# First and last groups of the prompt attention placed among the dense products beside them

## The chip, the cores and the metric

The kernel runs on one core of a Trainium2 chip. The metric is the device time of one execution in microseconds (us). The kernel before takes 2291.44 us, the median of 3 runs (2286.28 to 2295.47). One execution was also profiled; every instruction of that execution is in its trace.

## What is computed

The reference is one step of a decoder with two layers. It takes a prompt of 2048 tokens (width 1024) and a sample of 8 sequences of 4 new tokens each, whose past of 2048 tokens lies in a paged cache of keys and values (128 pages of 128 tokens, 4 heads of 128).

```
h   = rmsnorm(x)
a   = HGRN2(h)            # gated linear recurrence, 4 heads of 128
b   = forgetting attention(h)   # 4 heads of 128
x1  = x + concat(a * silu(ga), b * silu(gb)) @ w_out_even      # layer 0
x2  = x1 + GLA(rmsnorm(x1)) @ w_out_odd                        # layer 1
y   = rmsnorm(x2)
# forgetting attention of the prompt, per head, query t and key s <= t:
logits = q.k * scale + c[t] - c[s]        # c: running sum of log forget values
out    = softmax(logits) @ v
# of the sample: the same against the pages of its own past and its own new rows
```

The outputs are y for prompt and sample, the new keys, values and log forget values, and the final states of the two recurrences.

## The kernel before, in words

**Products.** A float32 product is made of three f16 products (`mm3`, L623 to L627): high by high, high by low, low by high. `act` is the large buffer with the left operand, split into a high and a low f16 part. A dense unit is one slice of a projection, 256 columns wide, for half of the prompt (1024 tokens, `hf` 0 or 1) and the sample's few rows. In the token-major form (`proj_tm`, L638) a unit has four steps of two token tiles each, called pairs: a pair is 2 tiles by 8 pieces of the contraction by 3, 48 products into a PSUM tile `pt_...`. A last small step treats the sample's few rows.

**Stages.** `phase_even` (L1118) makes the projections of layer 0. For each half it runs 16 units through `staged` (L1262); the last two are the keys Bk1 and the values Bv1 of the attention. Values leave PSUM by an eviction into `Bvs` (L1070), which the SP queue stores to DRAM as `vd` (L1084). At each step of the units `ahead` (L1551) does a step of the sample's work on cached keys: the list `KEYS` says at which steps 1 MB of key pages (`kp`, four loads at L1522, with their page numbers read into registers by `TENSOR_LOAD` at L1514) is loaded on SP; two and three steps later DVE transposes it (`kt`, L1526), then PE makes the scores, and SP stores them (`scd`). When the half changes, eight transposing loads on SP bring the second half's normalised rows into `act` (`act<-xhl`, L535).

`phase_fox` (L1347) is the attention. `fox_prompt` (L1365) goes through 16 groups (h, G): head h, 512 queries G, over the keys 0 to 512(G+1). SP loads what a group needs (L1379 on: `q`, `k`, the row `cb` of running sums from `cbd`, `v`, the gate `fsg`). Then, for each 128 queries: PE scores `s` (L625 to L627), DVE adds the bias and takes the maximum (`mx`, L1412), ACT takes the exponential into `L` (L1420), POOL scales it (L1428), PE transposes it (`pt<-ident,L`, L1448), ACT and DVE split it into the f16 parts `th` (L1455) and `tl` (L1456), and PE multiplies it with the values (`fo`). The finished output is stored to DRAM as `yT` (L1473), from POOL's queue. `fox_sample` (L1598) does the sample's attention over the cached values: 128 loads of 256 KB (`pgcache_fox_v`) and 34 products steps `pv` (L1750).

`phase_odd` (L2040) begins with layer 0's output projection. A unit of it needs a 256-column slice of the weight, loaded raw as `wr_o` and split into `w_o` (`half_unit`, L325: lines L356, L359, L362 and L363), and the left operand: `yT` read back from DRAM in pieces of 256 tokens (`y_pieces`, L1828; 1 MB each into the buffers `yr`, of which there are two), scaled and split into `act` by ACT, POOL and DVE (L1847 to L1854). The first half's pieces 0 to 3 come from the groups G = 0 and 1, so they do not wait for the last group (3,3).

**What sets the order.** The stages are generators that yield their cost. `until(a, ta, b, tb)` and `mux` alternate two of them so that each has done the same share of its total; `until` ends with the second, and `mux` with both. In `phase_fox` the prompt (total 270000) and the sample (500000) alternate so. What is left of the prompt alternates by `mux` with `prepare()` (L2119), which loads the first output unit's weights, splits them, and splits the pieces 0 and 1. Only then the attention's pools are closed and the output units run (`dense(0, 3)`). From this program order a scheduler lays out each engine's own instruction stream, within the dependencies; the streams then run in order on the chip.

## Time and profile before

| | us |
|---|---|
| median of 3 runs | 2291.44 |
| the profiled execution | 2291.65 |
| span of its trace, first to last instruction | 2289.9 |
| last even unit's products (Bv1) end, prompt's scores begin | about 911.4 |
| sample's transposed output `ys` (end of the sample) | about 1202.4 |
| end of the prompt's last group, first output unit begins | about 1229 |

The profile is of that one execution. PE is the matrix engine (PEld its weight loads, which run beside it), DVE the vector engine, ACT the scalar engine, POOL the general-purpose engine, SP the queue that issues most DMAs. A row of the timeline gives the start, the length, the engine, the line, the operation and its output and input; in square brackets stands how long the engine sat idle before it, and on whom it waited. A row of the waits gives the sum, the count and the longest. Successive matrix products overlap, so that a product shown as 0.27 us long can start 0.11 us after the one ahead of it. PEclk is the clock that was granted to PE, as a share of full speed.

### The profile page before, as it was taken

What the parts mean: (1) busy time and instruction counts of PE and PEld (TensorE: products, weight loads), DVE (VectorE), ACT (ScalarE), POOL (GpSimd) and SP (SyncE); (2) the same over time, 40 slices, a digit from 0 to 9 for tenths busy, and PEclk for the clock granted to TensorE, in tenths of its full rate; (3) what the DMA queues carried; (4) which work ended last, traced back from release to release, by engine and by line L of the source; (5) the groups of instructions that cost most, each with busy time, mean ns of one, the idle gap of its engine ahead of it and who ended that gap; (6) DMA issues with size and microseconds to landing.
All of it is one profiled execution on the core that took longest, in us unless ns stands there. A gap on an engine that the chain in (4) does not pass through costs nothing.

```text
span 2289.9 us, 58071 instructions
## 1 busy us (share of the span) xinstructions
PE 2195.9 (96%) x23316; PEld 1569.0 (69%) x23316; DVE 1400.7 (61%) x3154; ACT 994.3 (43%) x2216; POOL 724.9 (32%) x787
## 2 busy tenths in 40 slices
PE   7999999999999999899999999999999999999998
PEld 5667667774575588455457888677677667567887
DVE  7767677735564466877776454366665655557454
ACT  5434434321221221566667353554644644555243
POOL 2233234100110111544445354154442422232232
PEclk9999999999999999999999999999999999999999
DMA  7444545796575475977735779324325421115554
GB/s 235 144 124 150 160 150 185 233 238 151 159 184 138 118 204 149 280 223 246 223 111 170 260 219 253 101 71 144 92 97 101 120 79 59 54 52 179 171 179 152
DMA packets 361984, 364.02 MB, mean 159 GB/s; under 512 B 108161, under 2 KB 305090, under 8 KB 357490
## 3 DMA queue, kind: packets, MB, share of 16 engines
q1 hardware_dynamic: 359570, 353.69, 52.7%
q0 software_dynamic: 2144, 6.62, 0.8%
q8 instruction: 183, 3.00, 0.6%
q14 instruction: 87, 0.71, 0.1%
HBM read 245.85 MB, written 97.47 MB: 150 GB/s over the span
## 4 chain that ended last, share of the span: by engine, by line
PE 42%; DVE 3%; ACT 2%; DMA 2%; POOL 2%; issue 1%; SPq 0%; POOLq 0%; DVEq 0%; ACTq 0%
PE pt_o L625 4%; PE pt_o L626 4%; PE pt_o L627 4%; PE pt_Cv L625 2%; PE pt_Cv L627 2%; PE pt_Cv L626 2%; PE o_C L909 1%; PE gl_C L756 1%; PE pt L1448 1%; POOL s_C L842 1%; PE py_C L728 1%; ACT L L1420 1%; DMA wr_o<-in_w_out_odd 1%; PE fo L626 0%; PE fo L627 0%
## 5 line engine op out<-in xcount | busy, mean ns | idle before, releaser
L625 PE MATMUL pt_o<-w_o,act 128*128 128x256 f16 x1024 | 279.4, 273 | 1.4 <-ACT sg1C L682 1.4
L626 PE MATMUL pt_o<-w_o,act 128*128 128x256 f16 x1024 | 279.7, 273 | 0.0
L627 PE MATMUL pt_o<-w_o,act 128*128 128x256 f16 x1024 | 279.3, 273 | 0.0
L625 PEld LDWEIGHTS <-act 128*128 128x128 f16 x2304 | 226.1, 98 | 42.3 <-issue 5.3
L626 PEld LDWEIGHTS <-act 128*128 128x128 f16 x2304 | 226.3, 98 | 31.3 <-issue 2.2
L627 PEld LDWEIGHTS <-act 128*128 128x128 f16 x2304 | 226.1, 98 | 31.4 <-issue 2.6
L789 POOL TENSOR_TENSOR kA<-kA,fA 128x512 f32<-128x512 f32 (+1 forms) x56 | 74.2, 1325 | 367.9 <-PE gl_A L756 307.5
L625 PE MATMUL pt_Cv<-w_Cv,act 128*128 128x256 f16 (+1 forms) x512 | 141.5, 276 | 0.9 <-DVE rh L1959 0.8
L627 PE MATMUL pt_Cv<-w_Cv,act 128*128 128x256 f16 (+1 forms) x512 | 141.4, 276 | 0.0
L626 PE MATMUL pt_Cv<-w_Cv,act 128*128 128x256 f16 (+1 forms) x512 | 141.3, 276 | 0.0
L1420 ACT ACTIVATE L<-L,nm,kc 128x512 f32<-128x512 f32 (+3 forms) x160 | 118.2, 741 | 39.4 <-DVE nm L1418 36.1
L1428 POOL TENSOR_SCALAR L<-L,nm 128x512 f32<-128x512 f32 (+3 forms) x160 | 98.2, 629 | 87.4 <-DVE nm L1424 33.7
L789 POOL TENSOR_TENSOR kC<-kC,fC 128x512 f32<-128x512 f32 (+1 forms) x56 | 81.8, 1461 | 136.6 <-PE gl_C L756 93.1
L1455 ACT ACTIVATE th<-pt 128x512 f16<-128x512 f32 (+3 forms) x159 | 80.9, 526 | 74.1 <-PE pt L1448 73.4
L1526 DVE STREAM_TRANSPOSE kt<-kp 128x512 f32<-128x512 f32 x128 | 82.1, 684 | 40.7 <-DMA kp<-in_cache_fox_k 39.7
L1456 DVE TENSOR_TENSOR tl<-pt,th 128x512 f16<-128x512 f32 (+3 forms) x159 | 94.4, 607 | 16.0 <-ACT th L1455 15.0
L1448 PE MATMUL pt<-ident,L 128*128 128x128 f32 x544 | 89.8, 280 | 9.0 <-DVE tl L1456 5.6
L1448 PEld LDWEIGHTS pt<-ident,L 128*128 128x128 f32 x544 | 65.8, 143 | 39.1 <-DVE tl L1456 10.1
L788 DVE TENSOR_TENSOR qC<-qC,fC 128x512 f32<-128x512 f32 (+1 forms) x56 | 72.9, 1302 | 21.1 <-PE gl_C L756 21.1
L1950 ACT ACTIVATE vC<-pt_Cv,kc 128x512 f32<-128x512 f32 (+1 forms) x40 | 23.9, 598 | 134.0 <-PE pt_Cv L627 134.0
L625 PE MATMUL pt_Bv<-w_Bv,act 128*128 128x260 f16 (+1 forms) x256 | 70.8, 277 | 3.9 <-DVE Bvs L1070 3.9
L363 POOL TENSOR_TENSOR w_o<-wr_o,w_o 128x512 f16<-128x512 f32 x32 | 46.5, 1467 | 79.1 <-ACT w_o L362 55.2
(959 smaller groups left out, 6460.4 us busy)
## 6 DMA issues: line engine op xcount, KB each, us to landing
kp<-in_cache_fox_k SPq DMA_DIRECT2D x128, 256.0 KB, 4.9
pgcache_fox_v<-in_cache_fox_v SPq DMA_DIRECT2D x128, 256.0 KB, 4.1
yr<-yT SPq DMA_DIRECT2D x16, 1024.0 KB, 7.0
x1d<-xo SPq DMA_DIRECT2D x44, 256.0 KB, 4.1
wr_o<-in_w_out_even SPq DMA_DIRECT2D x32, 256.0 KB, 5.5
xo<-in_x_prompt SPq DMA_DIRECT2D x32, 256.0 KB, 4.5
wr_Cv<-in_w_in_odd SPq DMA_DIRECT2D x32, 256.0 KB, 3.4
x1r<-x1d SPq DMA_DIRECT2D x16, 512.0 KB, 4.5
```

The lines of the kernel that those rows point to most:

```text
L363: nc.gpsimd.tensor_tensor(lo, r, hi, ALU.subtract)
L625: nc.tensor.matmul(ps, lh[0], rh[0], start=first, stop=False)
L626: nc.tensor.matmul(ps, lh[0], rh[1], start=False, stop=False)
L627: return nc.tensor.matmul(ps, lh[1], rh[0], start=False, stop=last)
L788: nc.vector.tensor_tensor(xv[:, :, 1], xv[:, :, 1], t0.to_broadcast([P, nb, w]), ALU.mult)
L789: nc.gpsimd.tensor_tensor(kv[:, :, 0], kv[:, :, 0], t1.to_broadcast([P, nb, w]), ALU.mult)
L1420: self.last_exp = nc.scalar.activation(lt[:, :w], lt[:, :w], AF.Exp, bias=nm[:, 0:1], scale=ib, accum_out=nm[:, 2 + j : 3 + j])
L1428: nc.gpsimd.tensor_scalar(lt[:, :w], lt[:, :w], nm[:, 1:2], 2.0**14, ALU.mult, ALU.mult)
L1448: nc.tensor.transpose(pt[:, w : w + P], rows[b][s // 4][0][:, (s % 4) * P : (s % 4 + 1) * P], self.ident)
L1455: nc.scalar.activation(th[:, a:w], pt[:, a:w], AF.Copy),
L1456: nc.vector.tensor_tensor(tl[:, a:w], pt[:, a:w], th[:, a:w], ALU.subtract)))
L1526: return self.nc.vector.transpose(kt[:, :, 32 * x : 32 * x + 32], t[:, x].rearrange("p (a e) -> p a e", e=32))
```

## The change

Four things move.

- **Head.** The attention's pools are opened before the last even unit's four pairs are run. `drain(until(self.prompt, FOX_A, last, 21120.0))` then alternates the first 14000 of the prompt's cost with that unit's pairs. For that, the even phase's PSUM banks are split into two pools: the three banks `pj` of the running products stay, the others are closed, and five banks of the attention (`t`, `o`, `s`) take their place; the remaining three (`kt`, `sc`) open in `phase_fox`.
- **Key pages.** The `KEYS` list is changed: from the fifth of its 32 entries on each load comes four steps (one unit) earlier, and no key work is left in the unit Bv1; one of them now falls at the change of half.
- **Tail.** `prepare()` also runs the first output unit's four pairs, between the splits of the pieces 0 to 3, and loads and splits the second unit's weights. Their PSUM tiles use the attention's two `kt` banks. After the attention are left piece 4 (the sample's rows), the first unit's few-row step, and the units 1 and 2.
- **Shares.** The prompt has done some 14000 before the sample begins, and the sample is declared at 588000, so that it ends at an earlier point of the prompt, and more of the prompt is left for `mux` with `prepare` (43000 against 41500). In the sample a yield of 9000 stands ahead of the page sums. Transposes that run without other work alternate with the three `sc` banks and not the `kt` banks.

```diff
-REST_P = 18000.0
-REST_S = 12200.0
+REST_P = 43000.0
+REST_S = 41500.0
-KEYS = (*range(4 * 13, 4 * 17, 4), *range(4 * 17, 4 * 31, 2))
+KEYS = (4 * 13, 4 * 14, *range(4 * 15, 4 * 30, 2))
-FOX_S = 500000.0
+FOX_S = 588000.0
+FOX_A = 14000.0
...
-            drain(last)
-            for t in range(4 * 32, 4 * 32 + 2):
-                self.ahead(wpool, pps, t)
+            inner.close()
+            self.fox_open()
+            drain(until(self.prompt, FOX_A, last, 21120.0))
...
-                tag = "kt" if alone and j % 2 else "t"
+                tag = "sc" if alone and j % 2 else "t"
...
+            yield 9000
             tots = one([P, NH], "tots")
...
-                                   raw=("yr", 256) if (hf, layer, u) == (0, 0, 0) else ("wr", WU),
+                                   raw=("yr", 256) if (hf, layer) == (0, 0) and u < 2 else ("wr", WU),
...
+            banks, pps.pool, pps.bufs = pps.bufs, self.more_banks.pool, dict(pj="kt", gr="kt", o="kt", kt=2)
...
             def prepare():
                 units[0][0][0]()
                 pieces[0][0]()
                 yield 1
-                self.ready[0] = units[0][0][3]()
+                first = units[0][1](units[0][0][3]())
                 yield 4200
                 pieces[1][0]()
-                for steps in pieces[:2]:
-                    for step in steps[1:]:
-                        step()
-                        yield 1000
-
+                yield from splits(pieces[0])
+                pieces[2][0]()
+                yield next(first)
+                yield from splits(pieces[1])
+                pieces[3][0]()
+                yield next(first)
+                yield from splits(pieces[2])
+                units[1][0][0]()
+                yield next(first)
+                yield from splits(pieces[3])
+                self.ready[1] = units[1][0][3]()
+                yield 4200
+                yield next(first)
+                self.first = first
...
-            units[1][0][0]()
-
-            with tc.issue_after(self.turns[-1][0].ins):
-                for steps in pieces[2:]:
-                    for step in steps:
-                        step()
+            units[2][0][0]()
+            for step in pieces[4]:
+                step()
+            units[3][0][0]()
             with tc.issue_after(self.last_y.ins):
-                drain(dense(0, 3))
+                second = dense(1, 3)
+                next(second)
+                self.ready[2] = units[2][0][3]()
+                drain(self.first)
+                drain(second)
```

Line numbers after the change are one to nine higher (L625 becomes L626, L1384 becomes L1392). The rows below are each engine's instructions in its own order; the numbers behind a name tell one buffer's use from another's.

**Head, SP.** Before, in the stretch in which the last unit Bv ends, the loads of group (0,0) (`q_00`, `k_00`, `cb`, `v_00`, `fsg`) stand behind three stores of Bv's values (`vd_75<-Bvs`):

```order
L1325 DMA cbd<-cmask 64x128
L1084 DMA vd_75<-Bvs_12403 128x2x512
L1084 DMA vd_75<-Bvs_12484 128x2x512
L1564 DMA scd<-scs_12429 128x128
L1084 DMA vd_75<-Bvs_12545 128x2x512
L1384 DMA q_00_12659<-qd 128x2x512
L1386 DMA_TRANSPOSE k_00_12660<-kd_72 128x2x512
L1377 DMA cb_12664<-cbd 128x512
L1388 DMA v_00_12661<-vd_74 128x4x256
```

After, at the same place:

```order
L1329 DMA cbd<-cmask 64x128
L1392 DMA q_00_12421<-qd 128x2x512
L1394 DMA_TRANSPOSE k_00_12422<-kd_72 128x2x512
L1385 DMA cb_12426<-cbd 128x512
L1396 DMA v_00_12423<-vd_74 128x4x256
L1400 DMA fsg_12429<-sgd 128x512
L1392 DMA q_01_12504<-qd 128x2x512
L1085 DMA vd_75<-Bvs_12490 128x2x512
L1394 DMA_TRANSPOSE k_01_12505<-kd_72 128x2x512
```

The first group's loads and the query load of the second now stand ahead of the first store that waits for Bv. On PE the first scores accordingly stand in the middle of Bv's second pair (`pt_Bv_12627`), with the third (`pt_Bv_12746`) and the fourth behind them; before they stood behind the fourth:

```order
L626 MATMUL pt_Bv_12627<-w_Bv_11671,act 128x256
L626 LDWEIGHTS q_00_12421
L626 MATMUL s_12434<-k_00_12422,q_00_12421 128x128
...
L628 MATMUL s_12516<-k_00_12422,q_00_12421 128x256
L627 LDWEIGHTS act
L627 MATMUL pt_Bv_12627<-w_Bv_11671,act 128x256
...
L626 MATMUL pt_Bv_12746<-w_Bv_11671,act 128x256
```

What moved: the scores of groups (0,0) and (0,1) are spread over the last two and a half pairs of Bv.

**Tail, PE.** Before, the last `fo` products of the prompt's last group and then the first output unit's first pair (`pt_o`):

```order
L625 MATMUL fo_18062<-th_18286,v_33_17321 128x128
L626 LDWEIGHTS v_33_17321
L626 MATMUL fo_18062<-tl_18287,v_33_17321 128x128
L627 LDWEIGHTS v_33_17321
L627 MATMUL fo_18062<-th_18286,v_33_17321 128x128
L625 LDWEIGHTS act
L625 MATMUL pt_o_18379<-w_o_18006,act 128x256
```

After, some 600 rows ahead of the prompt's end, among the `fo` products of its last group but half:

```order
L627 MATMUL fo_17713<-tl_18055,v_32_17217 128x512
L628 LDWEIGHTS v_32_17217
L628 MATMUL fo_17713<-th_18054,v_32_17217 128x512
L626 LDWEIGHTS v_32_17217
L626 MATMUL fo_17713<-th_18065,v_32_17217 128x384
L628 LDWEIGHTS act
L628 MATMUL pt_o_17984<-w_o_17853,act 128x256
L626 LDWEIGHTS act
L626 MATMUL pt_o_17984<-w_o_17853,act 128x256
```

What moved: the 192 products of the first output unit's four pairs stand among the last 680 PE rows of the prompt.

**Tail, POOL.** The stream after, from the scaling of the first output weights to the split of piece 1 (`L` is the prompt's, `yr` and `act` a piece's, `w_o` the weight's):

```order
L360 TENSOR_SCALAR wr_o_17846<-wr_o_17846,kc 128x512
...
L1856 TENSOR_SCALAR yr_17851<-yr_17851,kc 128x512 x2
L364 TENSOR_TENSOR w_o_17853<-wr_o_17846,w_o_17853 128x512 x2
L1436 TENSOR_SCALAR L_17958<-L_17958,nm_18037 128x512
...
L1860 TENSOR_TENSOR act<-yr_17851,act 128x2x256 x2
L1436 TENSOR_SCALAR L_18089<-L_18089,nm_18112 128x512
...
L1856 TENSOR_SCALAR yr_17918<-yr_17918,kc 128x512 x2
```

In full it holds, up to the scaling of piece 1: two scalings of `wr_o`, one small mask, sixteen scalings of `L`, four scalings of `yr`, two splits of `w_o`, two splits of `act`. Before, the second piece's scaling also stood behind all the prompt's `L` rows.

**Change of half, SP.** Before, the fifth, sixth and seventh of the eight transposing loads of `act`, with stores between them:

```order
L535 DMA_TRANSPOSE act<-xhl 128x16x128
L1084 DMA vd_74<-Bvs_6407 128x2x512
L535 DMA_TRANSPOSE act<-xhl 128x16x128
L1087 DMA out_fox_v_p<-Bv_6470 128x2x256
L535 DMA_TRANSPOSE act<-xhl 128x16x128
```

After, behind the fifth:

```order
L1085 DMA vd_74<-Bvs_6413 128x2x512
L1522 TENSOR_LOAD scTs_886
L1522 ISA x8
L1530 ISA
L1530 DMA kp_6425<-in_cache_fox_k 32x4x512
...
L1530 DMA kp_6425<-in_cache_fox_k 32x4x512
L536 DMA_TRANSPOSE act<-xhl 128x16x128
L1085 DMA vd_74<-Bvs_6519 128x2x512
```

What moved: one megabyte of key pages stands ahead of the last three transposing loads; before it stood behind them and behind the next weight.

More of the change, by code (lines that the diff above doesn't have):

```diff
@@ L1345, in log_sigmoid @@
         nc.vector.scalar_tensor_tensor(zz, q, -2.0, zz, ALU.mult, ALU.add)
-    def phase_fox(self):
-        tc, nc = self.tc, self.nc
-        self.fox = ExitStack()
-        f1, f0 = (self.fox.enter_context(tc.tile_pool(name=x, bufs=2, reuse_waits="tile")) for x in ("fe", "fx"))
-        pp1, pp0 = (self.fox.enter_context(tc.tile_pool(name=x, bufs=2, space=PSUM, reuse_waits="tile"))
-                    for x in ("fpa", "fpb"))
-        if True:
-            fx = Pool(f0, {"P": 20},
-                      Pool(f1, {"caus": 1, "q2": 3, "k2": 6, "cb": 2, "st1": 12, "cm": 2, "th": 4, "tl": 4, "y": 1, "v2": 6, "sg": 3}))
-            pps = Pool(pp0, {"t": 2, "o": 1, "kt": 2}, Pool(pp1, {"s": 2, "sc": 1}))
-            caus = fx.tile([P, P], F32, tag="caus", name="caus")
-            nc.gpsimd.memset(caus, 0.0)
-            nc.gpsimd.affine_select(caus, caus, [[-1, P]], ALU.is_ge, FAR, base=0, channel_multiplier=1)
-            with tc.tile_pool(name="fs", bufs=1, side="right", reuse_waits="tile") as s0:
-                fs = Pool(s0, {"pg": PG, "kt": 2})
-                self.prompt = self.fox_prompt(fx, pps, caus)
-                drain(until(self.prompt, FOX_P, self.fox_sample(fs, pps), FOX_S))
@@ new lines, in fox_pool, with fox_open @@
+    def fox_pool(self, name, **kw):
+        return self.fox.enter_context(self.tc.tile_pool(name=name, bufs=2, reuse_waits="tile", **kw))
+    def fox_open(self):
+        nc = self.nc
+        self.fox = ExitStack()
+        f1, f0 = self.fox_pool("fe"), self.fox_pool("fx")
+        fx = Pool(f0, {"P": 20},
+                  Pool(f1, {"caus": 1, "q2": 3, "k2": 6, "cb": 2, "st1": 12, "cm": 2, "th": 4, "tl": 4, "y": 1, "v2": 6, "sg": 3}))
+        self.more_banks = Pool(None, {"kt": 2, "sc": 1})
+        self.fox_banks = Pool(self.fox_pool("fpa", space=PSUM), {"t": 2, "o": 1, "s": 2}, self.more_banks)
+        caus = fx.tile([P, P], F32, tag="caus", name="caus")
+        nc.gpsimd.memset(caus, 0.0)
+        nc.gpsimd.affine_select(caus, caus, [[-1, P]], ALU.is_ge, FAR, base=0, channel_multiplier=1)
+        self.prompt = self.fox_prompt(fx, self.fox_banks, caus)
@@ L1365, in fox_prompt @@
+    def phase_fox(self):
+        self.more_banks.pool = self.fox_pool("fpb", space=PSUM)
+        with self.tc.tile_pool(name="fs", bufs=1, side="right", reuse_waits="tile") as s0:
+            fs = Pool(s0, {"pg": PG, "kt": 2})
+            drain(until(self.prompt, FOX_P, self.fox_sample(fs, self.fox_banks), FOX_S))
     def fox_prompt(self, fx, pps, caus):
@@ L2116, in phase_odd, with splits @@
             self.ready, self.sam, self.early = {}, None, set()
-            pieces = self.y_pieces(0, 0, act, wpool, wp)
+            pieces = self.y_pieces(0, 0, act, wpool)
+            c2s.pool = late.enter_context(pool("c2", side="right"))
+            banks, pps.pool, pps.bufs = pps.bufs, self.more_banks.pool, dict(pj="kt", gr="kt", o="kt", kt=2)
+            def splits(p):
+                for step in p[1:]:
+                    step()
+                    yield 1000
             def prepare():
```

19 lines of the change are left out of this document (12 added, 7 removed).

## The prediction

> **What bounds the kernel now.** I read the page first: span, busy time and slices.
>
> ```profile
> span 2289.9 us, 58071 instructions
> PE 2195.9 (96%) x23316; PEld 1569.0 (69%) x23316; DVE 1400.7 (61%) x3154; ACT 994.3 (43%) x2216; POOL 724.9 (32%) x787
> PE   7999999999999999899999999999999999999998
> PE 42%; DVE 3%; ACT 2%; DMA 2%; POOL 2%; issue 1%; SPq 0%; POOLq 0%; DVEq 0%; ACTq 0%
> ```
>
> PE is busy in 96% of the span, and the chain that ended last runs over it more than over all the rest. The change takes no product away, so it can only win time in which PE stands idle or runs at a lower clock. The whole span has 2289.9 − 2195.9 = 94 us of idle PE. Where in the attention that time lies, the table of stretches tells. Its columns are the stretch, its length, and then the busy time of each engine, PE's clock, the DMA share and GB/s.
>
> ```profile
> core 0: us, PE busy (x) PEld busy (x) DVE busy (x) ACT busy (x) POOL busy (x), PEclk, DMA share, GB/s
> 911.40:930.60 19.20, 11.80 (x58) 5.59 (x58) 13.30 (x58) 8.76 (x23) 8.73 (x17) 0.82 1.05 295
> 916.00:922.00 6.00, 3.92 (x10) 1.17 (x9) 3.88 (x22) 2.42 (x7) 2.79 (x7) 0.51 1.14 333
> 970.00:1190.00 220.00, 212.94 (x1375) 114.85 (x1374) 168.96 (x584) 142.07 (x343) 98.17 (x175) 0.99 0.67 208
> 1211.00:1226.00 15.00, 10.26 (x44) 6.11 (x43) 11.43 (x23) 10.56 (x25) 12.41 (x14) 0.66 0.24 71
> 1216.00:1225.00 9.00, 7.52 (x29) 4.45 (x30) 5.92 (x15) 6.81 (x16) 6.41 (x8) 0.50 0.40 118
> 1240.00:1400.00 160.00, 160.00 (x1527) 141.16 (x1525) 78.94 (x95) 76.08 (x121) 75.27 (x50) 1.00 0.80 260
> ```
>
> Three things are to be seen. In the dense output units (1240 to 1400) PE is never idle. In the attention's middle (970 to 1190) it is idle for 7 us of 220. At the attention's two ends, 911.4 to 930.6 (the head) and 1211 to 1226 (the tail), it is idle for 7.40 of 19.20 and 4.74 of 15.00 us, and parts of both run at half clock. These ends are where the change puts dense products.
>
> **The change part by part: the head.** Whom PE waited for in 895 to 970 is in the waits; the timeline of PE, SP and POOL shows the order in which it came.
>
> ```profile
> PE s L625 <- DVE mx L1412: 6.7, 9, 2.6
> PE s L625 <- DVE Bvs L1070: 3.0, 1, 3.0
> ...
> 911.07 0.27 PE L626 MATMUL pt_Bv<-w_Bv,act 128*128 128x256 f16 x1
> 911.18 0.27 PE L627 MATMUL pt_Bv<-w_Bv,act 128*128 128x256 f16 x1
> 914.48 0.21 PE L625 MATMUL s<-k,q 128*128 128x128 f16 x1 [3.03 <-DVE Bvs L1070]
> ...
> 892.19 0.51 SPq L1325 DMA_DIRECT2D cbd<-cmask  x1
> 896.46 6.73 SPq L1084 DMA_DIRECT2D vd<-Bvs  x2
> 908.13 0.41 SPq L1084 DMA_DIRECT2D vd<-Bvs  x1
> 908.63 1.73 SPq L1384 DMA_DIRECT2D q<-qd  x1
> 911.85 0.51 SPq L1377 DMA_DIRECT2D cb<-cbd  x1
> ...
> 916.91 1.32 POOL L1398 TENSOR_TENSOR cm<-cb,caus 128x128 f32<-128x128 f32 x3 [3.64 <-DMA cb<-cbd]
> ```
>
> The first group's query load leaves SP only at 908.63. It was queued behind stores that waited for evictions of Bv (896.46 and 908.13), although the row it needs last, `cbd`, had been issued at 892.19. So `cb` goes out at 911.85, POOL makes the mask of it at 916.91, DVE's first maxima come behind that, and PE, with two `s` banks full, waits. The order after puts these loads behind `cbd`, ahead of the stores. Taking 892.19 as their start, they come 908.63 − 892.19 = 16.4 us sooner, and the chain from `cb` to the maxima runs while PE has Bv's third and fourth pair to do. That is 2 × 48 products at 0.11 us from start to start (911.07, 911.18) = 10.5 us.
>
> What can be won is the idle time, 7.40, and the half clock: 3.92 busy at a clock of 0.51 would be 1.96 at full speed, so 1.96. Together 9.36 us. Does the cover suffice? PE's own work in the new mixture is 10.5 + (11.80 − 1.96) = 20.3 us; DVE's 13.30 in the same stretch already holds the last evictions of Bv, POOL's is 8.73. Neither is longer than PE's. What I leave is one wait of about 1.4 us at the seam where Bv runs out and group (0,2) begins without cover, priced by the 1.6 us waits quoted for the tail below. Its waits beyond 930.6 stay. So the head gives −8.0, with bounds −9.4 and −3 (if only the 3.03 wait goes, and the chain itself, the waits on `mx`, still runs short). The stores of Bv now stand behind the loads; the groups that read what they store belong to the other two heads and come much later.
>
> **The tail.** Here the waits are on the chain inside the prompt's last group.
>
> ```profile
> PE pt L1448 <- DVE tl L1456: 4.0, 3, 1.6
> PE oT L1762 <- DVE oS L1759: 1.1, 1, 1.1
> ...
> 1215.97 0.66 PE L1448 MATMUL pt<-ident,L 128*128 128x128 f32 x2 [1.62 <-DVE tl L1456]
> 1216.43 0.64 PE L626 MATMUL fo<-tl,v 128*128 128x512 f16 x1
> ...
> 1213.49 1.73 DVE L356 SCALAR_TENSOR_TENSOR w_o<-wr_o,kc,w_o 128x512 f16<-128x512 f32 x1
> 1216.02 1.84 DVE L1854 SCALAR_TENSOR_TENSOR act<-yr,kc,act 128x512 f16<-128x512 f32 x2
> ```
>
> PE has no scores left and goes step by step with ACT and DVE, whose queues at the same time hold the splits of the first weights (1213.49) and pieces (1216.02). Removable are the idle 4.74 and the half clock, 7.52 × 0.5 = 3.76: together 8.5 us. The change puts the first unit's 192 products, 192 × 0.11 = 21 us of work without waits inside PE, in there. But each pair needs a piece that is split, and its splits are now to be done earlier, in between the prompt's `L`. POOL has the most of it:
>
> ```profile
> L1428 POOL TENSOR_SCALAR L<-L,nm 128x512 f32<-128x512 f32 (+2 forms) x12 | 8.2, 697 | 4.8 <-DVE tl L1456 2.6 <-ACT th L1455 2.2
> L1847 POOL TENSOR_SCALAR yr<-yr,kc 128x512 f32<-128x512 f32 x4 | 7.2, 1817 | 0.0
> L1851 POOL TENSOR_TENSOR act<-yr,act 128x512 f16<-128x512 f32 (+1 forms) x6 | 5.2, 870 | 4.5 <-ACT act L1850 4.5
> L359 POOL TENSOR_SCALAR wr_o<-wr_o,kc 128x512 f32<-128x512 f32 x2 | 3.1, 1562 | 0.0
> L363 POOL TENSOR_TENSOR w_o<-wr_o,w_o 128x512 f16<-128x512 f32 x2 | 2.3, 1158 | 0.0
> ```
>
> By the order after, up to the scaling of piece 1 POOL does 2 scalings of `wr_o` (3.1), 16 of `L` (16 × 0.697 = 11.2), 4 of `yr` (7.2), 2 splits of `w_o` (2.3) and 2 of `act` (1.7): 25.5 us in one string. PE's own work from 1211 to 1226 is 10.26 − 3.76 = 6.5 us at full clock, and with the first two pairs 6.5 + 10.5 = 17 us. By the order the first of the string stand two `L` groups earlier, ahead of this stretch, so the two are near to each other, and one or two waits of the size of the 1.62 are likely to be left, with part of the clock loss. I take −6.0 of the 8.5, leaving 2.5; bounds −8.5 and 0. The 1.1 of the sample's own transpose stays.
>
> The trace does show that such gaps cost clock: after idle times of 1.63 and 1.62 the product at 1216.43 takes 0.64 where the same form takes 0.38 in full clock, and 916 to 922 is at 0.51 behind the 3.03. [...]
>
> [...] In this trace the DVE split of a weight at 1213.49 takes 1.73, and the row below gives the spread for pieces:
>
> ```profile
> L1854 DVE SCALAR_TENSOR_TENSOR act<-yr,kc,act x54: 265/744/1599, 1216.0 to 2202.8; 128x512 f16<-128x512 f32 x48, 128x64 f16<-128x64 f32 x6
> ```
>
> The longest is 1599 ns at a median of 744. After the change the DVE splits of pieces 1 to 3 (three pieces of four steps, two of which go to DVE, 6 instructions) run beside POOL's scalings. At 1599 − 744 = 0.86 us more each that is 5 us on DVE, which has slack (11.43 of 15). Not in the sum, but in the second rival.
>
> **The change of half.** One megabyte of key pages now goes ahead of the last three transposing loads.
>
> ```profile
> 490.26 2.04 SPq L535 DMA_TRANSPOSE act<-xhl  x1
> 496.02 1.87 SPq L1522 DMA_DIRECT2D kp<-in_cache_fox_k  x4
> ...
> DMA to landing us min/median/max: 3.8/4.5/5.5
> ...
> L625 PE MATMUL pt_Av<-w_Ai,act x64: 270/273/284, 477.4 to 500.8; 128*128 128x256 f16 x64
> ...
> DMA packets 8802, 4.33 MB, mean 241 GB/s; under 512 B 7579, under 2 KB 8411, under 8 KB 8673
> ```
>
> The last of the loads leaves at 490.26 and lands 4.5 later, at 494.8. The 64 products run from 477.4 to 500.8, so the last eighth of them, which reads it, begins about 500.8 − 23.4/8 = 497.9: 3.1 us of cover. The key loads take 1.87 of SP and, at 241 GB/s, 1.05 MB / 241 = 4.3 us of the DMA engines: up to 6.2 later, 3.1 us too late. The queues share the bandwidth, so I take half, +1.5; bounds 0 and +3.1. The same loads leave room where they stood.
>
> **The middle.** The sample's steps now come on fewer rows of the prompt, so its cache loads come denser: 34 steps over 1585 PE rows in the order after against 1755 before, 10% more. The DMA share of 0.67 in 970 to 1190 becomes 0.74, still below one. PE's 7 us of idle time there might shrink or grow: 0, with ±3. The earlier key work costs the same operations in another unit: 0.
>
> **Sum.** −8.0 − 6.0 + 1.5 + 0 = −12.5. Against the profiled execution's 2291.65 (its span of 2289.9 and 1.75 around it; 0.2 above the median) that gives 2279.2 us. A change of about 0.5%, 11.5 us, is what a measurement of this kernel can tell from none; 2291.44 − 11.5 = 2279.98, so the forecast lies on that edge.
>
> **Rivals.** *All of it goes.* If the tail's cover suffices too, 9.4 + 8.5 = 17.9 go and nothing is paid at the change of half: 2273.8. With 3 won in the middle 2270.8. For it speaks that dense stretches are at 160.00 of 160.00; against it POOL's string of 25.5 us. Chance 0.17.
>
> *The tail gives it back.* The splits among the last group lengthen the very chain, `L` to `th` and `tl`, that PE waits for: POOL and DVE are at 12.41 and 11.43 of 15. Then the waits are only moved from `pt` to `pt_o`, and the 5 us of contention eats the cover: −8 + 0 + 1.5, 2285.2, or 2288.2 with 3 lost in the middle. Chance 0.18.
>
> *Slower, by the two `yr` buffers.* A piece's load takes 7.0 us and waits until a buffer is free:
>
> ```profile
> yr<-yT SPq DMA_DIRECT2D x16, 1024.0 KB, 7.0
> ```
>
> ACT and DVE take their instructions in order. If the split of piece 2 or 3 stands in their queues ahead of the last group's `th` and `tl` and its load has not landed, the prompt stops with it. Two such loads unhidden are 14.0, with the tail's half clock kept (no gain there), +1.5, and −8 for the head, with 3 lost in the denser middle: 2291.65 + 14.0 + 1.5 − 8 + 3 = 2302.2. It decides if a buffer comes free less than 7.0 us before its next pair's turn; a pair of 5.3 us alone does not cover a load, only pair and prompt work together do. Chance 0.10. That nothing moves at all is excluded by the order of the rows.
>
> **How the numbers follow.** The forecast has 0.55. Its edge at 2279.98 lies 0.8 above its centre, so half of it, 0.28, counts as faster and 0.27 as the same. Faster: 0.28 + 0.17 = 0.45. Same: 0.27 + 0.16 = 0.43. Slower: the third rival and a rest of the second, 0.10 + 0.02 = 0.12. For the range, 2270 takes in the first rival with all of the middle, and 2293 the second rival with the head at its bound of −3 (2288.2 + 5 = 2293.2); the third is left out.
>
> **What would show it.** Right: in the trace after, the idle time of PE between the end of Bk1 and group (0,2) is under 2 us with the clock at 1.0, `q` leaves SP some 16 us ahead of the last `vd`; and around the prompt's end the waits `pt<-tl` are gone, with `pt_o` waiting for `act` no more than 2.5. Wrong: waits of `s` on `mx` of over 4 us in the head (bound −3); waits of `pt_o` on `act` or `yr` of several us, or PEclk below 0.9 around the prompt's end (second rival); `th` or `tl` idle behind a piece's load (third); a `pt_Av` product waiting over 3 us on `act<-xhl`.

## The result, and the profile after

| kernel | median us | lowest to highest | runs |
|---|---|---|---|
| before | 2288.39 | 2284.10 to 2295.47 | 8 |
| changed | 2302.94 | 2300.65 to 2311.47 | 8 |

The changed kernel takes 1.0065 times as long as the kernel before, with a 95% interval of 1.005 to 1.008: some 15 us more. The forecast was 2279.2 us, 12 less than before. The profiled executions took 2291.65 us before and 2301.49 after; they lie 9.8 apart where the medians lie 14.6 apart, so the traces can account for two thirds of the difference.

The page of the changed kernel, with the rows that answer to those shown of before:

```profile
span 2299.8 us, 58075 instructions
PE 2192.9 (95%) x23316; PEld 1567.1 (68%) x23316; DVE 1391.3 (60%) x3154; ACT 993.1 (43%) x2216; POOL 726.9 (32%) x787
PE   7999998989999999899998999999999999999998
```

PE does the same 23316 products. A slice of this row is 57.5 us; in place of the nines of before there are eights in the seventh, ninth and twenty-second slice. The ninth, 460 to 517 us, is no part of the attention at all: it is the change of half. The direct way to find where time went is to set the same product in both traces side by side. Here are three such marks in each: the first product of the second half (`pt_Av`), the first of the unit behind its first two (`pf_A10f`), and the first product of the last even unit (`pt_Bv`), with the first of layer 1 (`pt_Cv`) as a fourth. PE's timeline of before:

```profile
477.44 0.28 PE L625 MATMUL pt_Av<-w_Ai,act 128*128 128x256 f16 x1
523.38 0.38 PE L625 MATMUL pf_A10f<-act,w_Aqf 128*128 128x512 f16 x1
887.78 0.28 PE L625 MATMUL pt_Bv<-w_Bv,act 128*128 128x256 f16 x1
1410.79 0.28 PE L625 MATMUL pt_Cv<-w_Cv,act 128*128 128x272 f16 x1
```

And of the changed kernel:

```profile
478.99 0.28 PE L626 MATMUL pt_Av<-w_Ai,act 128*128 128x256 f16 x1
540.52 0.38 PE L626 MATMUL pf_A10f<-act,w_Aqf 128*128 128x512 f16 x1
905.33 0.28 PE L626 MATMUL pt_Bv<-w_Bv,act 128*128 128x256 f16 x1
1420.89 0.28 PE L626 MATMUL pt_Cv<-w_Cv,act 128*128 128x272 f16 x1
```

Between two marks PE has the same products to do in both, but for the scores of the sample's keys (`ks`). The moved list puts four groups of 32 of them between the first two marks, where before had two, and none between the last two, where before had two; a group takes PE about 1.0 us. The **change of half** (first to second mark) takes 523.38 − 477.44 = 45.9 us before and 540.52 − 478.99 = 61.5 after: 15.6 more, 2 of them for the moved scores. Second to third mark is 364.4 and 364.8, with the same products. The **attention with its two ends and the output units** (third to fourth mark) takes 523.0 before and 515.6 after: 7.4 less, 2 of them for the moved scores, where the forecast had 14. So in these two executions the rearranged attention wins some 5 us, and more than twice as much is lost some 370 us ahead of it, where the key pages were moved.

### The profile page after: what moved, and what is told of

Read it like the earlier page. It is cut to its first block, busy times and chain, and to the rows that moved or that the text cites. A ratio compares the mean times of both kernels' runs of the same rounds, so it can differ in the third digit from the quotient of the medians.

```text
span 2299.8 us, 58075 instructions
## 1 busy us (share of the span) xinstructions
PE 2192.9 (95%) x23316; PEld 1567.1 (68%) x23316; DVE 1391.3 (60%) x3154; ACT 993.1 (43%) x2216; POOL 726.9 (32%) x787
## 4 chain that ended last, share of the span: by engine, by line
PE 39%; DMA 3%; DVE 3%; ACT 2%; POOL 2%; issue 1%; SPq 1%; POOLq 0%; DVEq 0%; ACTq 0%
PE pt_o L626 4%; PE pt_o L627 4%; PE pt_o L628 4%; PE pt_Cv L626 2%; PE pt_Cv L628 2%; PE pt_Cv L627 2%; DMA yr<-yT 1%; PE o_C L910 1%; PE gl_C L757 1%; PE pt L1456 1%; DMA wr_Cv<-in_w_in_odd 1%; SPq L338 1%; PE pv L1759 1%; POOL s_C L843 1%; PE py_C L729 1%
## 5 line engine op out<-in xcount | busy, mean ns | idle before, releaser
L626 PE MATMUL pt_o<-w_o,act 128*128 128x256 f16 x1024 | 279.6, 273 | 2.4 <-ACT sg1C L683 1.3
L626 PEld LDWEIGHTS <-act 128*128 128x128 f16 x2304 | 226.1, 98 | 47.5 <-issue 6.4
L626 PE MATMUL pt_Cv<-w_Cv,act 128*128 128x256 f16 (+1 forms) x512 | 140.8, 275 | 1.8 <-DMA act<-xs 1.8
L1534 DVE STREAM_TRANSPOSE kt<-kp 128x512 f32<-128x512 f32 x128 | 82.0, 684 | 48.2 <-DMA kp<-in_cache_fox_k 31.3
L626 PE MATMUL pt_Av<-w_Ai,act 128*128 128x256 f16 x256 | 71.7, 280 | 2.7 <-DVE Bvs L1071 1.4
L626 PE MATMUL pt_Bv<-w_Bv,act 128*128 128x260 f16 (+1 forms) x256 | 70.2, 274 | 3.9 <-DVE Bvs L1071 3.9
```

What stands on the lines that cost most here:

```text
L626: nc.tensor.matmul(ps, lh[0], rh[0], start=first, stop=False)
L1534: return self.nc.vector.transpose(kt[:, :, 32 * x : 32 * x + 32], t[:, x].rearrange("p (a e) -> p a e", e=32))
```

## The change of half in the two traces

SP's timeline of the changed kernel, then DVE's and PE's, and the waits of PE in 476 to 545:

```profile
487.96 1.89 SPq L1530 DMA_DIRECT2D kp<-in_cache_fox_k  x4
489.96 4.91 SPq L536 DMA_TRANSPOSE act<-xhl  x1
496.09 5.33 SPq L536 DMA_TRANSPOSE act<-xhl  x2
503.17 0.37 SPq L382 DMA_DIRECT2D w_Aqf<-wd  x1
505.71 8.74 SPq L1530 DMA_DIRECT2D kp<-in_cache_fox_k  x8
...
518.22 2.49 DVE L1534 STREAM_TRANSPOSE kt<-kp 128x512 f32<-128x512 f32 x4 [16.89 <-DMA scd<-scs]
...
520.76 1.94 PE L1579 MATMUL ks<-kt,qz 128*32 128x128 f32 x32 [8.33 <-DVE kt L1534]
...
PE ks L1579 <- DVE kt L1534: 9.0, 2, 8.3
PE pt_Av L626 <- DMA act<-xhl: 0.7, 1, 0.7
```

The same stretch of before, where the last transposing load of `act` went out at 490.26:

```profile
482.76 2.46 SPq L535 DMA_TRANSPOSE act<-xhl  x1
...
485.94 3.59 SPq L535 DMA_TRANSPOSE act<-xhl  x1
...
493.48 0.37 SPq L381 DMA_DIRECT2D w_Aqf<-wd  x1
...
504.27 2.49 DVE L1526 STREAM_TRANSPOSE kt<-kp 128x512 f32<-128x512 f32 x4 [18.83 <-DMA kp<-in_cache_fox_k]
...
PE ks L1571 <- DVE kt L1526: 1.0, 2, 0.6
```

The prediction's step asked one question: do the last transposing loads land before PE reads them? They nearly do: PE waits 0.7 for them. What it left out is the rest of SP's stream behind the megabyte. The next weight goes out at 503.17, 9.7 later than before. Of this, 2.3 were lost ahead of the megabyte (the fifth transposing load leaves at 481.80, before at 479.52). The megabyte costs SP not 1.87 us but 5.0, from 484.98, when the store ahead of it is out, to 489.96: 3.0 go by up to the first issue at 487.96, where the instructions that read the page numbers stand. The transposing load behind it takes 4.91 of SP's time, where the one at that place took 2.46, so 2.4 more. The last two take 5.33 together, and took 3.59 and 2.04 before. The next keys stand behind that weight. They go out from 505.71, together with the megabyte after them, and the first megabyte's last load lands at 518.0, 10.7 after it went out, where it was 6.6 before; DVE turns the keys at 518.22 (the row names `scd<-scs`, but the store of that name at 515.20 lands only at 522.3). The scores `ks` of these keys stand in PE's stream among the products of the unit Ag, which use the same weight and the same `act` ahead of the scores, up to 512.4, and behind them, from 522.63, without a wait. PE does not go on to those behind: it stands still for 8.33 us. Table of stretches of the changed kernel:

```profile
core 0: us, PE busy (x) PEld busy (x) DVE busy (x) ACT busy (x) POOL busy (x), PEclk, DMA share, GB/s
508.00:522.00 14.00, 5.67 (x45) 2.96 (x47) 3.06 (x5) 1.44 (x3) 0.00 (x0) 0.75 0.94 216
520.76:525.10 4.34, 4.34 (x38) 2.27 (x39) 1.83 (x3) 0.28 (x1) 0.00 (x0) 0.50 0.82 186
915.50:938.00 22.50, 21.45 (x169) 15.88 (x166) 17.07 (x66) 10.66 (x29) 11.12 (x21) 1.00 1.12 287
1217.00:1240.00 23.00, 16.64 (x117) 10.98 (x116) 14.16 (x32) 16.89 (x37) 21.24 (x22) 0.97 0.37 115
```

In the first two rows is the wait and the clock behind it: the wait of 8.33 is the idle time of the first row, and when PE goes on it is busy for 4.34 us at a clock of 0.50, some 2.2 lost by estimate, half of the 4.34. The other two rows are the head and the tail, read below.

## The experiments

Each run is compared with runs of the kernel before on the same chip. The ratio is to the kernel before, with its 95% interval; 0.001 is 2.3 us. The two stretches are those between the marks above, from each run's own profiled execution: "half" is `pt_Av` to `pf_A10f`, "attention" is `pt_Bv` to `pt_Cv`.

| run | key list | head | tail | ratio (interval) | half us | attention us |
|---|---|---|---|---|---|---|
| before | old | old | old | 1 | 45.9 | 523.0 |
| changed | new | new | new | 1.0065 (1.005 to 1.008) | 61.5 | 515.6 |
| before_keys | new | old | old | 1.0045 (1.0029 to 1.0061) | 56.2 | 520.8 |
| load62 | one load ahead | old | old | 1.0029 (1.0015 to 1.0044) | 55.9 | 520.8 |
| load66 | one load behind | old | old | 0.9998 (0.9981 to 1.0015) | 46.9 | 521.6 |
| keys_kept | 48 and 50 | new | new | 1.0037 (1.0025 to 1.0049) | 47.5 | 523.3 |
| head_only | 48 and 50 | new | old | 1.0007 (0.9992 to 1.0021) | 47.6 | 512.8 |
| tail_only | 48 and 50 | scores old | new | 1.0093 (1.0074 to 1.0111) | 49.0 | 530.3 |
| before_c3 | 99 and 107 | old | old | 1.0017 (1.0001 to 1.0032) | 45.2 | 521.9 |
| head_c3 | 99 and 107 | new | old | 0.9981 (0.9968 to 0.9994) | 48.1 | 513.3 |
| all_c3 | 99 and 107 | new | new | 1.0004 (0.9989 to 1.0018) | 48.2 | 523.6 |
| all_c3_cheap | 99 and 107 | new | new, cheap split | 0.9991 (0.9975 to 1.0007) | 47.1 | 510.5 |
| head_c3_cheap | 99 and 107 | new | old, cheap split | 0.9999 (0.9982 to 1.0015) | 48.0 | 519.3 |
| all_c3_noload | 99 and 107 | new | new, two loads less | 1.0013 (1.0000 to 1.0025) | 46.7 | 518.4 |
| tail_two | 99 and 107 | new | half of new | 1.0039 (1.0021 to 1.0056) | 47.0 | 526.6 |

One caution on the last columns: the attention's stretch holds two groups of key scores in before, one in load62 and load66, and none in the others. And runs with the same instructions in a stretch differ in it. The second half's units from `pf_A10f` on take 362.8, 365.8 and 370.5 us in keys_kept, head_only and tail_only, whose streams there are the same. A difference of under some 5 us in one execution is not read as an effect; a wait that returns at the same place in several is. The profiled execution can also lie far from its kernel's median: all_c3's took 2299.87 at a median of 2292.91, all_c3_cheap's 2281.62 at 2290.42, and head_c3_cheap's, the slowest of ten, 2298.77 at 2293.36.

**before_keys**: the new list alone.

```diff
-KEYS = (*range(4 * 13, 4 * 17, 4), *range(4 * 17, 4 * 31, 2))
+KEYS = (4 * 13, 4 * 14, *range(4 * 15, 4 * 30, 2))
```

> The kernel before with one edit: the changed kernel's list of key loads. Theory H: the key list by itself costs 15 to 18 us, 2304 to 2306, with PE waiting about 8 us for the transposed keys behind the change of half. Rival R, and the recorded prediction: 0 to 3 us.

Measured: 1.0045, 10 us more, with 56.2 us in the change of half. The list alone, with nothing of the attention moved, makes the kernel slower; the size is below the 15 to 18 expected, and far from 0 to 3.

**keys_kept, head_only, tail_only**: the changed kernel with another list, and then with one end only.

```diff
-KEYS = (4 * 13, 4 * 14, *range(4 * 15, 4 * 30, 2))
+KEYS = (48, 50, 52, 56, 60, 64, *range(68, 120, 2))
...
# head_only: REST_P, REST_S, prepare() and what follows it as before, FOX_S = 547000
# tail_only:
-            drain(until(self.prompt, FOX_A, last, 21120.0))
+            drain(last)
-FOX_S = 588000.0
+FOX_S = 547000.0
```

> The changed kernel with one edit: the list of key loads keeps the steps 52, 56, 60, 64 and 68 of the kernel before around the change of half, and the two loads that this needs go to the steps 48 and 50. Theory H (the new list at the change of half costs some 15.6 us, and head and tail together give 7.5): the time falls by 15 to 17 us against the changed kernel, to 2285 to 2288, within 0.3% of the kernel before, and PE's first product of f_A10 stands at about 523 to 525 us as before, not at 540.5. Rival R (the loss sits in the tail, by the loads into the two yr buffers, and the change of half is only where this one profiled execution was late): it falls by less than 4 us, to 2299 or more.

> The changed kernel with the mended key list and the old tail (the old prepare, the output units' old order, the sample's declared cost at 547000 so that it ends where it did before in the prompt). Only the head differs from the kernel before. Theory H with a right head term: 8 us below the kernel before, 2279 to 2282. If the head only moves its waits: 2286 to 2289.

> The changed kernel with the mended key list, and the last even unit run to its end before the prompt's products begin (the loads of the prompt's first groups may still go out sooner). Only the tail differs from the kernel before in what PE does. Theory H (the tail takes back with idle time what it wins in clock): within 2 us of the kernel before, 2286 to 2290. The recorded prediction's term: 6 us below, 2282. Rival R: 5 or more above, 2293 or more.

Measured: 1.0037, 1.0007 and 1.0093. The change of half is mended (47.5 to 49.0 us), but the time did not come back to 2285 to 2288: my sum for keys_kept was wrong. Head and tail together do not give 7.5; with the old tail the run is 0.0030 or 7 us faster. head_only is no faster than the kernel before, where 8 less was expected. One reason is in the list with 48 and 50: in these three traces the first mark stands at 482.88, 483.36 and 484.99 against 477.44, and 2 us of that are two groups of key scores that now come ahead of it. That list was not run with both old ends, so the three can be compared only with each other. So theory H held for the place of the largest loss and failed for the tail, which I had put at zero. tail_only, 5 us or more above as the rival said, is the slowest run of all; but its head is not quite that of before, since the prompt's loads still go out sooner there.

**load62, load66**: in the kernel before, one load moved, to tell what in the new list does the harm.

```diff
-KEYS = (*range(4 * 13, 4 * 17, 4), *range(4 * 17, 4 * 31, 2))
+KEYS = (52, 56, 60, 62, 64, *range(68, 122, 2))    # load62
+KEYS = (52, 56, 60, 64, 66, *range(68, 122, 2))    # load66
```

> The kernel before with one key load moved: the list has a load at step 62 (in the last unit of the first half) and none at 122. On SP one megabyte of keys then stands ahead of the last three transposing loads, as in the changed kernel; behind the change of half the loads stay four steps apart up to 68. Theory H1 (the loss at the change of half comes from the megabyte ahead of the transposing loads: they land late, and with them the weight and key loads queued behind): PE loses 6 us or more between the first product of the second half and f_A10, where the kernel before loses 1.7. Theory H2 (it comes from the two megabytes too many behind it, which share the bandwidth with the weights): less than 4 us there.

> The kernel before with one key load added at step 66 and none at 122: nothing new stands ahead of the transposing loads, but the loads behind the change of half come two steps apart from 64 on. H1: PE loses 1.7 to 4 us in the same stretch, as before. H2: 6 us or more.

The marks in load62:

```profile
481.14 0.28 PE L625 MATMUL pt_Av<-w_Ai,act 128*128 128x256 f16 x1
536.99 0.38 PE L625 MATMUL pf_A10f<-act,w_Aqf 128*128 128x512 f16 x1
...
PE ks L1571 <- DVE kt L1526: 5.4, 2, 4.7
PE pt_Av L625 <- DMA act<-xhl: 1.8, 2, 1.6
```

And in load66:

```profile
479.21 0.28 PE L625 MATMUL pt_Av<-w_Ai,act 128*128 128x256 f16 x1
526.10 0.38 PE L625 MATMUL pf_A10f<-act,w_Aqf 128*128 128x512 f16 x1
...
PE ks L1571 <- DVE kt L1526: 1.1, 2, 0.6
```

Measured: 1.0029 and 0.9998; 55.9 against 46.9 us in the stretch, where the kernel before has 45.9. Both runs have the same products there, one group of key scores more than before, and that group is the 1 us of load66. A megabyte ahead of the three transposing loads costs 9 us more than behind them (by the times 0.0031, 7 us) and brings the wait of `ks` on `kt` of 4.7; behind them it brings none, though it comes at the same density as in the new list. This decides for H1 and against H2. In before_keys, which has the whole new list, the longest such wait is 4.2, so the 8.33 of the changed kernel's trace is not the rule. The load at 62 is the fourth entry of the new list, which before stood at 64; the description of the change begins with the fifth.

**head_c3, all_c3, before_c3**: a list that leaves the change of half as it was and makes up for the loads at 120 and 122 in the second half; with the new head and old tail, with both new, and by itself in the kernel before.

```diff
-KEYS = (4 * 13, 4 * 14, *range(4 * 15, 4 * 30, 2))
+KEYS = (52, 56, 60, 64, *range(68, 99, 2), 99, *range(100, 107, 2), 107, *range(108, 119, 2))
```

> The changed kernel's head with the old tail, and a key list that is the kernel before's up to step 68 and makes up for the two loads at 120 and 122 with extra loads at 99 and 107. The list with 48 and 50 lost 3 to 6 us in the first half; if that was the early keys, and the head gives 8 to 9: 7 to 9 us below the kernel before, a ratio of 0.996 to 0.997. If any list that frees the last unit costs what the head gives: within 3 us.

> The whole change (head and tail) with the same key list, extra loads at 99 and 107. Theory T (the tail costs 5 to 7 us against the old tail): 2 to 4 us below the kernel before, and 5 to 7 above the run with the head alone. The recorded prediction without its wrong key term: 14 below.

> The kernel before with the mended key list alone (as before up to step 68, extra loads at 99 and 107, none at 120 and 122). The run with this list and the new head was 0.9981 of the kernel before, 4.4 us below. If the head is worth the recorded 8 us, the list by itself costs 3 to 4: 2294 to 2297, a ratio of 1.0015 or a little above. If the list is free: within 0.0010 of 1, and the head is worth 4.

Measured: 0.9981, 1.0004, 1.0017. The list by itself costs 0.0017, 3.9 us; list and head together win 0.0019, 4.4 us, where 7 to 9 were expected. The head is therefore worth 0.0036 or 8.2 us. The attention's stretch says the same: 513.3 against 521.9, 8.6 less. Adding the new tail takes 0.0023, 5 us, away, so that all_c3 is no faster than the kernel before, where 2 to 4 less was expected. And all_c3 differs from the changed kernel in the key list alone: 1.0065 − 1.0004 = 0.0061, 14.0 us. head_c3 is faster than both kernels, at 2288.31 against 2291.93 in its comparison, and its interval excludes 1.

**all_c3_cheap, head_c3_cheap, all_c3_noload, tail_two**: why the tail gives nothing.

```diff
# all_c3_cheap and head_c3_cheap, in split(k):
+                if (layer, hf, c0) == (0, 0, 0):
+                    self.last_y = nc.scalar.activation(h2, r2, AF.Copy, scale=sy)
+                    nc.vector.memset(l2, 0.0)
-                if layer == 0 and k in YPOOL:
+                elif layer == 0 and k in YPOOL:
# all_c3_noload, in load():
+                if (layer, hf, c0) == (0, 0, 0) and s >= 512:
+                    t["raw"] = self.raws[s - 512]
+                    return
...
+                if (layer, hf, c0) == (0, 0, 0):
+                    self.raws[s] = t["raw"]
# tail_two, in prepare():
                 yield from splits(pieces[0])
-                pieces[2][0]()
                 yield next(first)
                 yield from splits(pieces[1])
-                pieces[3][0]()
                 yield next(first)
...
-FOX_S = 588000.0
+FOX_S = 560000.0
```

> The run all_c3 with the split of the first output half's four prompt pieces made cheap: ACT writes the scaled high part, and the low part is set to zero by DVE. The low part of that operand is left out of the computation, and with it all of POOL's and most of DVE's work on it. Theory C (the splits crowd the prompt's last groups on ACT, POOL and DVE, so that the waits are only moved): PE's lost time from the end of the sample to the first product of the second layer falls from 18 us (13.6 and a gap of 4.6) by at least 5. Rival W (the waits are those of the prompt's own chain, or of the loads into the two yr buffers): it falls by less than 3.

> The same cheap split in the kernel with the new head, the mended key list and the old tail; again the low part of the operand is left out. Under theory C the old tail, which splits two pieces among the last group, gains less than the new one: 1 to 4 us of its 11.2. If it gains as much as the new tail, the splits are not what sets the two apart.

> The run all_c3 without the loads of pieces 2 and 3: they are split from the data of pieces 0 and 1, so their rows of the operand are wrong, and all the splitting work stays. If the waits for the loads into the two buffers are what the tail costs: PE's lost time from the end of the sample to the second layer falls from 18 to 12 or less, ratio 0.998. If it is the splitting work: it stays above 15, ratio 1.000.

> New head, mended key list, and a smaller tail: only the first output unit's first two pairs stand among the prompt's last groups, behind the splits of pieces 0 and 1 that stood there before; pieces 2 and 3, the other pairs and the second unit's weights come behind the prompt. Theory C: the same splits as in the old tail, with 10.5 us of products to fill its waits, so 2 to 5 us below head_c3, a ratio of 0.996 to 0.997. If the waits are of the chain itself or of the changed order of the loads: as head_c3, 0.998, or above.

The waits of PE in the tail of all_c3, 1189 to 1290, and its first product of layer 1:

```profile
PE fo L626 <- ACT th L1463: 2.4, 2, 1.3
PE pt L1456 <- DVE tl L1464: 2.2, 4, 0.8
PE pt L1456 <- DVE nm L1426: 1.8, 1, 1.8
PE s L626 <- DVE mx L1420: 1.1, 1, 1.1
...
1417.91 0.41 PE L626 MATMUL pt_Cv<-w_Cv,act 128*128 128x272 f16 x1 [4.41 <-DMA act<-xs]
```

The waits in the tail of head_c3, which has the old tail:

```profile
PE pt L1456 <- DVE tl L1464: 3.1, 4, 1.3
PE fo L626 <- ACT th L1463: 2.4, 2, 1.3
PE fo L627 <- DVE tl L1464: 1.8, 2, 1.4
```

And those of all_c3_cheap:

```profile
PE pt_o L626 <- ACT act L1855: 2.5, 1, 2.5
PE pt_o L627 <- POOL w_o L364: 1.5, 1, 1.5
PE pt L1456 <- DVE tl L1464: 0.6, 1, 0.6
```

Measured: 0.9991, 0.9999, 1.0013 and 1.0039. The two cheap kernels leave out the low part of the first half's operand, and all_c3_noload two of its four loads. With the cheap split the waits of `fo`, `s` and of `pt` on `nm`, which are the prompt's own chain, are gone. PE's idle time from the end of the sample to the first product of layer 1 is 13.5 us in all_c3, 4.9 with the cheap split and 12.3 without two loads. By the traces, then, the splitting work matters to these waits and the loads hardly do; but 4.4 of the 8.6 less are the wait for `act<-xs` at the end of that stretch, which the cheap split happens to lose. By the times neither is shown: 0.9991 and 1.0013 against 1.0004 lie within their intervals of each other, and the profiled executions of all_c3 and all_c3_cheap lie 18 us apart where the ratios lie 0.0013, 3 us, apart.

Two runs went against theory C. head_c3_cheap should have gained, and did not: 0.9999, with an interval that overlaps that of head_c3. In its profiled execution, the slowest of ten, PE waits 5.4 us in one place for `th`, and ACT in the same stretch waits 6.6 for a piece (`yr<-yT`). Shorter splits seem to have let the order put a piece's work ahead of the prompt's `th` in ACT's stream, with the load not there yet; this is read from one trace and was not tested. tail_two should have been the best and is 13 us slower than head_c3; its stretch is 526.6 against 513.3, with the sample's share of the prompt also set otherwise, so that it cannot be put down to the pairs.

## Why the prediction was wrong, step by step

- **The change of half, +1.5 with bounds 0 and +3.1: the step that failed most.** The new list costs 10.3 us where it is the only edit (before_keys, whose stretch here is 10.3 longer), and 14.0 between two kernels that differ in the list alone (all_c3 and the changed one). The prediction said that "The last of the loads leaves at 490.26 and lands 4.5 later" and compared this with PE's last need of it. It priced the moved megabyte by SP's 1.87 and its bandwidth, and by one reader. That shared bandwidth would halve the price was my estimate, and no run shows it; PE waits 0.7 for the transposing loads in the changed kernel's trace and 1.8 in that of load62. SP lost 5.0 to it and 2.4 more at the load behind it, and the step did not follow the two things queued behind: the weight of the next unit but one, 9.7 us late, and the next keys, for which PE waits 8.33 with other products behind. load62 against load66 (55.9 us in the stretch against 46.9) shows that the place ahead of the transposing loads does it.
- **"The earlier key work costs the same operations in another unit: 0."** Not shown wrong for the new list: between its second and third marks it takes 364.8 against 364.4. But it does not hold for any list. The one with 99 and 107 costs 3.9 us by itself (1.0001 to 1.0032), and its stretch of the second half's units takes 369.6 to 374.2 in all seven traces; two groups of key scores more, some 2 us, are part of that.
- **The head, −8.0: right.** 8.2 us (head_c3 against before_c3). From the first product of Bv to the 46th product of the prompt's scores, in group (0,2), the six traces with the old head take 42.7 to 46.6 us, up to 2 of them for key scores, and the nine with the new one 35.3 to 37.1. The wait of 3.03 ahead of the first score is in five of the six (not in tail_only, where the loads go out sooner) and in none of the nine. But the priced wait on `mx` belongs in part to the key list: it is 6.7 before and 1.3 in before_c3, where the list alone has taken the key work out of Bv. In the changed kernel's trace `q` leaves SP at once behind `cbd`, and the table of stretches above shows 915.5 to 938 with 1.05 us of idle time and the clock at 1.00, where 911.4 to 930.6 had 7.40 and 0.82. What is left are waits at the seam:

```profile
909.41 0.50 SPq L1329 DMA_DIRECT2D cbd<-cmask  x1
910.00 0.57 SPq L1392 DMA_DIRECT2D q<-qd  x1
...
938.71 0.39 PE L626 MATMUL s<-k,q 128*128 128x512 f16 x1 [1.76 <-DVE mx L1420]
```

  The 1.76 there is the one wait that was left in the sum, at the place that was named, 1.4 by the estimate; with two smaller ones on `mx` it is 2.7. It came 0.7 us behind 938 and so is not in the row of 915.5.
- **The tail, −6.0 with bounds −8.5 and 0: wrong, outside its bounds.** It cost 5 us (all_c3 against head_c3; 7 between keys_kept and head_only). The step that failed is that the first unit's products would fill the waits and that "one or two waits of the size of the 1.62 are likely to be left". Half of the term came true: the clock is 0.97 in the 23 us from 1217, against 0.78 in the 23 us from 1207 before. The waits stayed. From the end of the sample to the first product of layer 1, in before, changed, head_c3 and all_c3:

```profile
1199.10:1410.79 211.69, 206.73 (x1868) 177.19 (x1867) 113.21 (x179) 105.54 (x187) 107.01 (x86) 0.98 0.71 223
1200.30:1420.89 220.59, 212.13 (x1914) 180.33 (x1912) 111.13 (x201) 110.79 (x200) 111.08 (x92) 0.99 0.68 217
1194.40:1405.45 211.05, 202.76 (x1851) 174.97 (x1850) 109.62 (x176) 102.27 (x179) 106.21 (x85) 0.99 0.71 226
1190.30:1417.91 227.61, 214.15 (x1913) 181.35 (x1911) 114.01 (x202) 110.91 (x200) 110.89 (x93) 0.98 0.68 211
```

  The stretches begin at different points of the prompt, so their lengths do not compare, but PE's idle time does: 5.0, 8.5, 8.3 and 13.5. With the new head, then, the prompt's waits are as large with the new tail as with the old one: 13.5 less the 4.4 for `act<-xs` is 9.1, against 8.3. The second rival foresaw that the chain would be lengthened, with a price of zero; that the waits move to `pt_o` did not happen, since `pt_o` waits only 1.4 there. Its 5 us of contention did not come either: the six DVE splits of pieces 1 to 3 took 4.9 us in all in the changed kernel's trace, 0.5 above six times the median of 744 ns. The traces do show such splits longer beside POOL: in before the 31 of 128x512 with POOL idle took 0.73 to 0.75 us, and the 11 with POOL busy for over half of their time 0.73 to 1.60, 0.96 on average. That POOL is crowded by the new splits is not shown: it is busy 21.24 of the 23 us from 1217, but 20.40 of 23 from 1207 to 1230 before. The cost is for the most part the 4.4, at a place that the prediction did not look at. SP's queue in all_c3, its wait, and the first of the transposing loads for layer 1 in head_c3:

```profile
1407.56 0.37 SPq L830 DMA_DIRECT2D s_C<-in_state_gla  x1
...
1408.54 16.10 SPq L595 DMA_TRANSPOSE act<-xs  x5
...
SPq L830 <- DMA x1d<-xo: 4.5, 1, 4.5
...
1395.08 4.37 SPq L595 DMA_TRANSPOSE act<-xs  x1
```

  In all_c3 a load of a state (`s_C`) waits 4.5 us on SP for a store to land, and the transposing loads stand behind it. In head_c3 the first of them stands ahead of that load and goes out 10.4 us before its reader. The same wait of SP is 3.0 to 5.4 us in all seven kernels that run products of the first unit in `prepare`, and 0.9 or less in the eight others; PE's wait behind it is 0.9 to 4.4 in the seven, 1.8 in the changed kernel's trace. It is the change of half's mistake once more, a load queued behind another, but no run was made with that order alone.
- **The third rival** came out with nearly the measured time, 2302.2 against 2302.9, by luck: it starts from 2291.65 where before's median is 2288.39, and its reason is not the measured one. In the changed kernel ACT waits for pieces, as it said, but PE's waits for `th` behind them are small, 2.0 in all:

```profile
ACT act L1862 <- DMA yr<-yT: 8.5, 4, 3.1
```

  Its 14 us of unhidden loads did not happen here. The trace of head_c3_cheap has the mechanism once, at 5.4 us.
- **The middle, 0 ± 3**: not settled. The mixed waits differ by a few us among runs in both directions, and tail_two may be such a case.
- **The clock.** I took it from the trace of before that gaps of about 1.6 us cost clock. The later traces show it both ways. In the changed kernel it was 0.75 in 508 to 522 around the wait of 8.33, and 0.51 in 1238.5 to 1242, behind waits of 0.40, 0.96 and 0.43 (1235.86, 1237.43 and 1239.15). But it was 1.00 in 938.7 to 945, with waits of 1.76 and 0.71 (938.71 and 940.63), and 1.00 in 1222.7 to 1226, behind one of 1.77. In head_c3 it was 0.50 in 928.5 to 931.9, behind waits of 1.76 and 0.71. What sets the clock is not shown.

The measured steps from the kernel before to the changed one are the list with 99 and 107, +0.0017; the head, −0.0036; the tail, +0.0023; and the new list in that one's place, +0.0061. They make 0.0065, as they must, being steps of one chain; their agreement with the measured ratio is no check of it. In the prediction's terms: head −8.2 where −8.0 was forecast, tail +5.3 where −6.0 was, and the key list +17.9 by this chain, or +10.3 alone, where +1.5 was.

**What stays open.** Whether the list really costs more with the new ends (17.9 in the chain) than with the old ones (10.3), and why. How the tail's 5 us divide between the prompt's waits and the wait for `act<-xs`; the traces give most of it to the second, and the times do not separate them. Why the attention's stretch is 515.6 in the changed kernel and 523.3 and 523.6 in keys_kept and all_c3, with the same head and tail.

## What to carry to other kernels

When a change moves a load to another place in a queue, follow everything queued behind it to its readers, and look in each reader's own stream for what stands in order behind that reader; here the load that was moved was not the one that was missed. A list that is only rearranged to make room for the change is part of the change, and deserves its own run: here the part that was meant to win did win, and the housekeeping cost more. Before filling an engine's waits with other work, ask whether the chain that it waits for gets any shorter by that, and follow what the new order does to the queues behind the filled stretch.

## What the runs showed of the hardware

A transposing load issued directly behind four loads of 256 KB held SP for 4.91 us in the changed kernel (5.10 in before_keys, 5.26 in load62), where the last five of the kernel before took 2.04 to 3.59; why it does is not shown. In the changed kernel a weight load of 1 MB issued into the same stretch landed after 10.4 to 11.0 us, against 5.7 to 7.2 before, at 216 GB/s and a DMA share of 0.94 in 508 to 522. In the same trace SP spent 3.0 us (484.98 to 487.96) on the instructions that read the page numbers ahead of one megabyte of key loads, and 1.9 on issuing it. And the same instruction stream took 362.8, 365.8 and 370.5 us for the same units in three executions (keys_kept, head_only and tail_only), so that a single profile does not settle a few microseconds.
